# Hybrid decoder block on one core: softmax of query tiles placed between value products, two heads' operands in SBUF

## Chip, cores and metric

The kernel runs on one core of one Trainium2 chip. The metric is device time in microseconds (us), the median of several executions. One further execution was taken with the hardware profiler; the views quoted below come from it. Engines carry the profile's names: PE is TensorE (PEld its weight load), DVE VectorE, ACT ScalarE, POOL GpSimd, SP the engine that issues most DMAs.

## The reference, cut to what matters

One decoder block on 1024 tokens and 1024 channels, in fp32. After a norm and an input projection, two branches run side by side, are gated, merged and projected, and a gated ConvFFN follows. The change touches the stage in which both branches are computed.

```
# forgetting attention (FoX), 8 heads of 128
s = q_t . k_s * scale + (c_t - c_s)          # c: running sum of log forget gates; causal
o = softmax(s) @ v
# gated DeltaNet, 8 heads, in 8 chunks of 128 tokens here
S_t = exp(g_t) (I - beta_t k_t k_t^T) S_{t-1} + beta_t k_t v_t^T ;  o_t = S_t^T q_t
```

## The kernel before

The program is a row of stages: input projection with Strassen-like block products (`project`), the mixing stage (`mix`), the merge of the branches (`merge`), the output projection (`mix_out`), the ConvFFN. Products in fp32 are made of three products of high and low parts (`hi*hi`, `hi*lo`, `lo*hi`), so each operand is first split: ACT writes the high part as a cast, and POOL or DVE subtracts it to leave the low part.

In `mix` (L1276) a generator `fox` (L1246) emits the attention, one head after the other, in small steps; between its steps the loop at L1438 emits steps of two scan streams (`stream`, L1405; even heads and odd heads) and of the preparation of scan inputs (`prep`, L1287). PE follows the order in which the code is written (`manual_schedule` for PE). The other engines and the DMA queue of SP are ordered by a scheduler at build time, except where `keep_in_program_order` pins an instruction. Every engine runs its own queue in order.

A head of the attention has 8 query tiles of 128 rows, t = 0 to 7.

- `probs(h, t)` (L1174) makes one tile of probabilities. PE multiplies query and keys (three matmuls, L1187 to L1189) into a PSUM tile of `small()`; DVE adds the bias row, `cr` or, on the diagonal block, the masked `cd`, and keeps the running maximum (L1194, a pair of instructions each time); DVE negates it (L1200), ACT takes the exponential with the row sum (L1201), DVE inverts the sum and scales the tile (L1202, L1203). For t below 4 there is one score chunk, for t of 4 and more two of equal width (320, 384, 448 and 512 columns).
- `attend(h, half)` (L1206) multiplies four tiles of probabilities with the values. For each key block j, PE transposes the blocks (L1224) into a tile of `small()`, ACT and DVE split the result into `ph` and `pl` (L106, L107), and PE makes the three products with `vh`, `vl` (L1215), two key blocks later. Half 0 has 4 key blocks and tiles 0 to 3, half 1 has 8 key blocks and tiles 4 to 7.

`small()` hands out four PSUM tiles in turn, to scores, transposes, scan preparation and scan output alike. The order of a head (L1253 to L1273) is: all eight `probs`, the attend steps of half 0, then those of half 1. The four early tiles of head 0 are made in the projection (`EARLY`, L85). One set of query and key tiles (`qh`, `ql`, `kh`, `kl`), one of bias rows (`cr`, `cd`, 1024 wide) and one `vl` serve all heads. Loads of the next head's query, keys and bias are written at the first step of half 0; their split (`fox_query`, `fox_key`, L1124 to L1136) at steps 1 and 4 of half 1; the values are loaded after half 1 and split (`fox_values`, L1138) after the first chunk of tile 4.

`prep(h)` for a scan head loads eleven inputs and scales two of them on POOL (L1320: `svt` by `brk`, `skt` by `dkl`) in its first step; two further steps make the inverse's off-diagonal block (L1325 to L1333). The first `prep` is emitted at step 0 of `fox`, the scan streams begin at steps 12 and 21. In `stream` the `prep` of the next head but one is taken at steps 14, 18 and 21 of the scan.

The pool `stream2`, which holds three 512 KB tiles `wr` for weights, opens before `mix` (L449); SP loads the first three tiles of the output projection's weights into it at the start of the mixing stage.

Of the kernel before, what the change touches and what calls it, by code (L numbers as in the profile page):

```python
# [9 lines left out]
F32 = mybir.dt.float32  # L10
# [77 lines left out]
class Block:  # L88
# [322 lines left out]
    def run(self):  # L411
# [5 lines left out]
        with ExitStack() as ctx:  # L417
# [31 lines left out]
            self.st = pool(ctx, "stream2", side="right")  # L449
# [13 lines left out]
            self.mix([pool(left, f"fox{i}") for i in range(4)], pool(sc, "scan", side="right"), merge_pools)  # L463
# [11 lines left out]
            bs.close()  # L475
            banks(2, 6)
# [78 lines left out]
    def head_in(self, blk, right):  # L555
# [3 lines left out]
        with tc.tile_pool(name="hin", bufs=1) as pool, ExitStack() as px:  # L559
# [96 lines left out]
            for t in range(NT):  # L656
# [12 lines left out]
                if t == NT - 2:  # L669
# [6 lines left out]
                                   ("t2", "t3", "t1")))  # L676
# [444 lines left out]
    def fox_load_values(self, h):  # L1121
        self.fox_load(self.vl, self.vd[:, h * P:(h + 1) * P].rearrange("(t p) d -> p t d", p=P))

    def fox_query(self):  # L1124

        self.fox_parts(self.qh, self.ql)

    def fox_key(self):
        self.fox_parts(self.kh, self.kl)
# [8 lines left out]
    def fox_values(self):  # L1138
        raw = self.vl.bitcast(F32)
        self.nc.gpsimd.tensor_copy(self.vf, raw[:, 3::4, :])  # L1140
        for sl in (slice(0, 4), slice(4, 8)):

            self.tc.keep_in_program_order(self.nc.scalar.copy(self.vh[:, sl], raw[:, sl]))
            self.nc.gpsimd.tensor_tensor(self.vl[:, sl], raw[:, sl], self.vh[:, sl].bitcast(F32), ALU.subtract)

    def fox_bias(self, h):
        nc = self.nc
        nc.sync.dma_start(self.cr, self.rows_d[(H + h) * NT:(H + h + 1) * NT, :].rearrange("t c -> (t c)")
                          .partition_broadcast(P))
        nc.gpsimd.affine_select(out=self.cd.rearrange("p (n c) -> p n c", n=NT),  # L1150
                                in_=self.cr.rearrange("p (n c) -> p n c", n=NT),
                                compare_op=ALU.is_ge, fill=NEG, base=0, pattern=[[0, NT], [-1, P]],
                                channel_multiplier=1)

    def fox_first(self, pool):

        self.fox_in = pool
        self.qh, self.ql, self.kh, self.kl = (pool.tile([P, S], F32R, name=n) for n in ("qh", "ql", "kh", "kl"))
        self.cr, self.cd = (pool.tile([P, S], F32, name=n) for n in ("cr", "cd"))
        self.vl = pool.tile([P, NT, P], F32R, name="vl")  # L1160
        self.fox_load(self.ql, self.q_d[0])
        self.fox_load(self.kl, self.k_d[0])
        self.fox_bias(0)
        self.fox_load_values(0)
        yield
# [884 lines left out]
```

## Time and profile before

| | |
|---|---|
| time, median of 3 runs | 1992.53 us (1988.59 to 1996.03) |
| time of the profiled execution | 1994.26 us |
| its span | 1992.6 us |
| PE, DVE, ACT, POOL busy in the span | 96%, 75%, 54%, 48% |
| mixing stage in the span | about 812 to 1066 us |

The windows view gives, for a stretch of the span, the busy time of each engine with the count of its instructions, the clock that PE was granted as a share of full speed, the share of time in which DMA engines moved data, and GB/s. The groups view has one row per line, engine and tile: busy time, mean ns of one instruction, then the engine's idle time just before and what ended it. A timeline row is start, duration, engine, line, operation and tile. Matmuls are pipelined: the profile's duration of one is longer than the distance to the next.

### The profile page before, as it was taken

What the parts mean: (1) busy time and instruction counts of PE and PEld (TensorE: products, weight loads), DVE (VectorE), ACT (ScalarE), POOL (GpSimd) and SP (SyncE); (2) the same over time, 40 slices, a digit from 0 to 9 for tenths busy, and PEclk for the clock granted to TensorE, in tenths of its full rate; (3) what the DMA queues carried; (4) which work ended last, traced back from release to release, by engine and by line L of the source; (5) the groups of instructions that cost most, each with busy time, mean ns of one, the idle gap of its engine ahead of it and who ended that gap; (6) DMA issues with size and microseconds to landing.
All of it is one profiled execution on the core that took longest, in us unless ns stands there. A gap on an engine that the chain in (4) does not pass through costs nothing. (4 is left out here: it accounts for less than half of the span.)

```text
span 1992.6 us, 29214 instructions
## 1 busy us (share of the span) xinstructions
PE 1920.6 (96%) x9674; PEld 1605.2 (81%) x9674; DVE 1492.4 (75%) x2549; ACT 1067.5 (54%) x2383; POOL 954.3 (48%) x792
## 2 busy tenths in 40 slices
PE   8999999999999999999998999999999999999998
PEld 8988887888887777788886887877788888877886
DVE  6949887867999974487887797668877676778435
ACT  5436776763334445476765443466555555553234
POOL 2845656555555455455655043154665656530012
PEclk9999999999999999899999999999999999999999
DMA  5335556565323366766665743573433434378654
GB/s 166 96 101 164 174 189 188 185 211 206 112 106 111 112 213 257 259 222 212 230 219 203 231 137 131 188 242 124 163 126 112 148 118 136 118 250 319 211 195 160
DMA packets 191608, 350.89 MB, mean 176 GB/s; under 512 B 50784, under 2 KB 79712, under 8 KB 191456
## 3 DMA queue, kind: packets, MB, share of 16 engines
q1 hardware_dynamic: 190448, 345.35, 51.2%
q10 hardware_dynamic: 1008, 3.67, 0.5%
q8 instruction: 76, 1.25, 0.3%
q14 instruction: 76, 0.62, 0.1%
HBM read 232.76 MB, written 116.20 MB: 175 GB/s over the span
## 5 line engine op out<-in xcount | busy, mean ns | idle before, releaser
L107 POOL TENSOR_TENSOR ol<-ws,oh 128x512 fp32r<-128x512 f32 x212 | 288.3, 1362 | 218.4 <-ACT oh L106 207.6
L107 POOL TENSOR_TENSOR ol<-wr,oh 128x512 fp32r<-128x512 f32 x165 | 230.4, 1399 | 271.0 <-ACT oh L106 213.9
L106 ACT CAST oh<-ws 128x512 fp32r<-128x512 f32 x212 | 131.0, 618 | 178.3 <-PE mm L159 172.4
L106 ACT CAST oh<-wr 128x512 fp32r<-128x512 f32 x201 | 121.5, 615 | 107.7 <-PE mm L159 74.2
L205 DVE TENSOR_TENSOR ws<-wr 128x512 f32<-128x512 f32 x106 | 99.1, 935 | 103.2 <-DMA wr<-in_w_up_dram 70.5
L390 DVE SCALAR_TENSOR_TENSOR cv<-c,fw,cv 128x512 f32<-128x512 f32 (+2 forms) x176 | 127.5, 748 | 10.0 <-ACT cv L385 8.5
L390 DVE SCALAR_TENSOR_TENSOR cv<-c,cw,cv 128x511 f32<-128x511 f32 (+2 forms) x144 | 105.9, 748 | 7.4 <-ACT cv L385 5.8
L1038 DVE TENSOR_TENSOR invt<-invz 128x399 f32<-128x399 f32 (+50 forms) x114 | 94.7, 845 | 0.3
L264 ACT COPY x<-mm 128x512 f32<-128x512 f32 x158 | 91.7, 581 | 4.5 <-PE mm L159 4.5
L159 PE MATMUL mm<-b22h,oh 128*128 128x512 f32 x216 | 86.1, 399 | 7.4 <-ACT x L264 7.3
L159 PE MATMUL mm<-bt1h,oh 128*128 128x512 f32 x216 | 85.2, 395 | 5.1 <-ACT x L264 5.1
L107 DVE TENSOR_TENSOR ol<-wd,oh 128x512 fp32r<-128x512 f32 x66 | 46.3, 706 | 57.5 <-ACT oh L106 57.4
L159 PE MATMUL mm<-bt4h,oh 128*128 128x512 f32 x216 | 84.8, 393 | 4.4 <-DVE c L311 4.4
L159 PE MATMUL mm<-b11h,ol 128*128 128x512 f32 x216 | 86.2, 399 | 0.7 <-POOL ol L107 0.7
L159 PE MATMUL mm<-b11h,oh 128*128 128x512 f32 x216 | 85.8, 397 | 1.0 <-ACT oh L106 1.0
L159 PE MATMUL mm<-b11l,oh 128*128 128x512 f32 x216 | 86.4, 400 | 0.0
L159 PE MATMUL mm<-b22l,oh 128*128 128x512 f32 x216 | 86.0, 398 | 0.0
L159 PE MATMUL mm<-b21l,oh 128*128 128x512 f32 x216 | 86.0, 398 | 0.0
L159 PE MATMUL mm<-bt4l,oh 128*128 128x512 f32 x216 | 85.7, 397 | 0.0
L159 PE MATMUL mm<-bt2l,oh 128*128 128x512 f32 x216 | 85.1, 394 | 0.3 <-DVE bt2l L107 0.3
L159 PE MATMUL mm<-bt1l,oh 128*128 128x512 f32 x216 | 84.9, 393 | 0.0
L159 PE MATMUL mm<-b21h,oh 128*128 128x512 f32 x216 | 84.9, 393 | 0.0
(426 smaller groups left out, 6381.0 us busy)
## 6 DMA issues: line engine op xcount, KB each, us to landing
wr<-in_w_up_dram SPq DMA_DIRECT2D x43, 512.0 KB, 3.6
wr<-in_w_gdn_dram SPq DMA_DIRECT2D x24, 512.0 KB, 3.8
wr<-in_w_out_dram SPq DMA_DIRECT2D x24, 512.0 KB, 3.9
s<-hy SPq DMA_DIRECT2D x44, 256.0 KB, 3.0
s<-z SPq DMA_DIRECT2D x44, 256.0 KB, 3.9
wd<-in_w_down_dram SPq DMA_DIRECT2D x44, 256.0 KB, 5.7
b22h<-s SPq DMA_DIRECT2D x44, 256.0 KB, 2.9
b22l<-s SPq DMA_DIRECT2D x44, 256.0 KB, 3.3
```

Source lines behind the costliest of these rows:

```text
L106: cast = nc.scalar.copy(hi, src)
L107: (lo_eng or nc.vector).tensor_tensor(lo, src, hi.bitcast(F32), ALU.subtract)
L159: self.nc.tensor.matmul(ps, lhs[:, sl], rhs[:, k, :], start=(first and k == 0 and i == 0), stop=(k == 3 and i == 2), skip_group_check=True)
L205: v.tensor_tensor(t, x, y, op)
L264: nc.scalar.copy(t, x)
L390: nc.vector.scalar_tensor_tensor(t[:, lo:], c[:, 512 * j + lo - s:512 * (j + 1) - s], w[:, n - 1 - s:n - s], t[:, lo:], op0=ALU.mult, op1= ...
L1038: nc.vector.tensor_tensor(tv, z[:, m:n, 0:n].to_broadcast([P, r, n]), z[:, m, c0:c1].unsqueeze(2).to_broadcast([P, r, n]), ALU.mult))
```

## The change

Five things change.

1. A head is written in one list of 26 steps: half 0's value products with the late tiles' softmax (t = 4 to 7) between them, then half 1's value products, with the next head's early tiles (t = 0 to 3) ahead of them and among them. Chunks of scores are 512 columns and the rest, which for t = 4 is 512 + 256 computed columns (128 used) and one bias instruction fewer. A tile's last part (maximum, exponential, scaling) now belongs to the step of its last score chunk.
2. Two sets of query, key and value tiles stand in SBUF, for even and odd heads, the second in a pool of its own (`other`). The bias is in halves: the lower one per set, the upper one (`crh`) and the two masked ones (`cd`) single.
3. Loads and splits of the next head move to steps 1, 3 and 5 of the 26, beside the late tiles; the split of the head's own values to step 2 (step 0 for head 0).
4. In `prep` the loads are a step of their own; POOL's scaling is the next step, and pinned in program order. The streams take `prep` at scan steps 10, 15, 18 and 21; the first stream begins at step 9, the second at step 19.
5. `stream2` opens after the merge's last pool is closed, and the three block tiles of the projection stand in another order in their pool.

```diff
-            self.st = pool(ctx, "stream2", side="right")
...
             bs.close()
+            self.st = pool(ctx, "stream2", side="right")
...
-                                   ("t2", "t3", "t1")))
+                                   ("t1", "t2", "t3")))
...
+    def fox_load_head(self, h):
+        _, ql, _, kl, _ = self.sets[h % 2]
+        self.fox_load(ql, self.q_d[h])
+        self.fox_load(kl, self.k_d[h])
+        self.fox_bias(h, 0)
...
-        w = n if t < 4 else n // 2
...
-        for lo in range(0, n, w):
+        for half, lo in enumerate(range(0, n, 512)):
...
         nc.vector.tensor_scalar(p, p, mm[:, 1:2], None, op0=ALU.mult)
         pts.append(p)
+        yield
...
         for h in range(H):
-            pts = [] if h else self.pts
-            for t in range(len(pts), NT):
-                yield from self.probs(h, t, pts)
-                if h and t == 4:
-                    self.fox_values()
-            for half in range(2):
-                for i, _ in enumerate(self.attend(h, half, pts)):
...
+            late, early = late(), early()
+            order = [first, late, late] * 4 + [first, early, early, early, last, last, last, early] + [last] * 6
+            for i, part in enumerate(order):
+                if i == 1 and more:
+                    self.fox_load_head(h + 1)
+                    self.fox_load_values(h + 1)
+                elif i == 3 and more:
+                    self.fox_query(h + 1)
+                elif i == 5 and more:
+                    self.fox_key(h + 1)
+                if i == (2 if h else 0):
+                    self.fox_values(h)
+                if next(part, DONE) is not DONE:
+                    yield
+                if i == 12:
+                    finish(first)
+                    if more:
+                        self.fox_bias(h + 1, 1)
...
-                eng = nc.gpsimd
+                yield
                 for t, f in ((vb, self.brk), (kt, self.dkl)):
                     for sl in (slice(0, 4), slice(4, 8)):
-                        eng.tensor_tensor(t[:, sl], t[:, sl], bc(f)[:, sl], ALU.mult)
+
+                        tc.keep_in_program_order(
+                            nc.gpsimd.tensor_tensor(t[:, sl], t[:, sl], bc(f)[:, sl], ALU.mult))
                 yield
...
-                        if h + 2 < H and i in (14, 18, 21):
-                            if i == 14:
+                        if h + 2 < H and i in (10, 15, 18, 21):
+                            if i == 10:
```

What this does to the queues, at three places. First PE, within a head of the steady state (the third). `p_` tiles under `ident` are transposes of probabilities for the value products, `kh,qh` and its two companions are scores, `us` are the scan. Before, the last two tiles' scores and the first transposes behind them:

```order
L1187 MATMUL ms<-kh,qh 128x448
L1188 MATMUL ms<-kl,qh 128x448
L1189 MATMUL ms<-kh,ql 128x448
L1357 MATMUL us<-ss,sqd 128x128
L1358 MATMUL us<-su,saq 128x128
L1351 MATMUL us<-sr,sxt 128x128
L1325 MATMUL ms<-sx_9190,sat 64x64 x8
L1187 MATMUL ms<-kh,qh 128x512
L1188 MATMUL ms<-kl,qh 128x512
L1189 MATMUL ms<-kh,ql 128x512
```

In the changed kernel, the same head's half 0 and its first late tile:

```order
L1242 MATMUL ms<-ident,p_9036 128x128
L1242 MATMUL ms<-ident,p_9083 128x128
L1242 MATMUL ms<-ident,p_9096 128x128
L1242 MATMUL ms<-ident,p_9156 128x128
L1203 MATMUL ms<-kh,qh 128x512
L1204 MATMUL ms<-kl,qh 128x512
L1205 MATMUL ms<-kh,ql 128x512
L1392 MATMUL us<-ss,sqd 128x128
L1393 MATMUL us<-su,saq 128x128
L1381 MATMUL us<-ss,skT 128x128
L1203 MATMUL ms<-kh,qh 128x256
L1204 MATMUL ms<-kl,qh 128x256
```

Scores used to follow scores with only scan work between; now each tile's scores stand between the transposes of two key blocks.

Second POOL, at the entry of the mixing stage, from the split of head 0's values on. `ql`, `kl` are the low parts of head 1's query and keys, `svt` and `skt` the scan inputs, first those of scan head 0. Before:

```order
L1144 TENSOR_TENSOR vl<-vl,vh 128x512 x2
L1320 TENSOR_TENSOR svt<-svt,brk 128x512 x2
L1320 TENSOR_TENSOR skt<-skt,dkl 128x512 x2
L1136 TENSOR_TENSOR ql<-ql,qh 128x512 x2
L1150 AFFINE_SELECT cd<-cr 128x1024
```

In the changed kernel:

```order
L1145 TENSOR_TENSOR vl<-vl,vh 128x512 x2
L1136 TENSOR_TENSOR ql<-ql,qh 128x512 x2
L1136 TENSOR_TENSOR kl<-kl,kh 128x512
L1153 AFFINE_SELECT cd_7828<-crl 128x512
L1355 TENSOR_TENSOR svt<-svt,brk 128x512 x2
L1355 TENSOR_TENSOR skt<-skt,dkl 128x512 x2
```

The scan inputs of head 0 used to be scaled ahead of head 1's query; now they stand behind head 1's query, half its keys and its masked bias.

Third SP at the same place: the last loads of scan head 0 and what follows. Before:

```order
L1293 DMA sqd<-qdd_1551 128x1024
L1378 DMA sgz<-gzd_1592 128x1024
L126 DMA wr<-in_w_out_dram 128x1024 x3
L1119 DMA kl<-kd_1585 128x1024
L1119 DMA ql<-qd_1577 128x1024
```

In the changed kernel:

```order
L1326 DMA sqd<-qdd_1551 128x1024
L1119 DMA ql<-qd_1577 128x1024
L1119 DMA kl<-kd_1585 128x1024
L1152 DMA crl<-rows 128x512
L1119 DMA vl<-vd 128x8x128
L1413 DMA sgz<-gzd_1592 128x1024
```

Head 1's query and keys move up by four transfers; the three weight tiles `wr` left this place for the middle of the merge.

More of the change, by code (lines that the diff above doesn't have):

```diff
@@ L461, in merge_pools @@
                 self.merge_first(pool(bs, "br0"))
-            self.mix([pool(left, f"fox{i}") for i in range(4)], pool(sc, "scan", side="right"), merge_pools)
+            self.mix([pool(left, f"fox{i}") for i in range(5)], pool(sc, "scan", side="right"), merge_pools)
             sc.close()
@@ L1155, in fox_first, with bias, fox_set @@
+    def bias(self, h, half):
+        return (self.crh if half else self.sets[h % 2][4]), self.cd[half]
+    def fox_set(self, pool):
+        return ([pool.tile([P, S], F32R, name=n) for n in ("qh", "ql", "kh", "kl")]
+                + [pool.tile([P, 512], F32, name="crl")])
+    def fox_load_head(self, h):
[3 more added lines that the diff above has]
+        self.fox_bias(h, 0)
     def fox_first(self, pool):
         self.fox_in = pool
-        self.qh, self.ql, self.kh, self.kl = (pool.tile([P, S], F32R, name=n) for n in ("qh", "ql", "kh", "kl"))
@@ L1159, in fox_first @@
[L1159 to L1163, printed above, removed]
+        self.sets = [self.fox_set(pool)]
+        self.crh = pool.tile([P, 512], F32, name="crh")
+        self.cd = [pool.tile([P, 512], F32, name=f"cd{i}") for i in range(2)]
+        self.vls = [pool.tile([P, NT, P], F32R, name="vl")]
+        self.fox_load_head(0)
@@ new lines, in fox, with late, early @@
+            more, after = h + 1 < H, []
+            first, last = self.attend(h, 0, pts), self.attend(h, 1, pts)
+            def late():
+                for t in range(4, NT):
+                    yield from self.probs(h, t, pts)
+            def early():
+                for t in range(4 if more else 0):
+                    yield from self.probs(h + 1, t, after)
+            late, early = late(), early()
+            order = [first, late, late] * 4 + [first, early, early, early, last, last, last, early] + [last] * 6
@@ L1276, in mix @@
+            for part in (first, late, early, last):
+                finish(part)
+            pts = after
     def mix(self, fp, pool, before_last):
@@ L1449, in mix @@
                             take(s, 1)
[L1450 removed]
+                elif i >= 9 and i % 2:
                     take(streams[0], 1)
```

88 lines of the change are left out of this document (41 added, 47 removed).

## The prediction

> **What bounds the kernel now.** I read the page first, then stretches of the mixing stage in the windows view, then the waits of PE, then rows of the groups and the timeline.
>
> ```profile
> PE 1920.6 (96%) x9674; PEld 1605.2 (81%) x9674; DVE 1492.4 (75%) x2549; ACT 1067.5 (54%) x2383; POOL 954.3 (48%) x792
> ```
>
> PE is busy in 1920.6 of 1992.6 us, so over the whole span a change can win 72 us at most. Its instructions change order in the mixing stage alone. The next rows cut that stage into its entry and its remainder, and three heads of the remainder at the place where the softmax ends. The columns are length, then busy time of PE, PEld, DVE, ACT, POOL, then PE's clock.
>
> ```profile
> core 0: us, PE busy (x) PEld busy (x) DVE busy (x) ACT busy (x) POOL busy (x), PEclk, DMA share, GB/s
> 811.90:842.60 30.70, 26.73 (x173) 22.46 (x172) 18.83 (x53) 15.11 (x34) 15.27 (x14) 0.83 0.98 337
> 842.60:1065.60 223.00, 210.07 (x1570) 191.15 (x1568) 179.58 (x639) 156.87 (x502) 123.33 (x133) 1.00 0.60 204
> ...
> 904.40:923.50 19.10, 17.58 (x123) 15.85 (x123) 18.39 (x78) 13.83 (x46) 4.85 (x5) 1.00 0.62 207
> 923.50:937.20 13.70, 12.99 (x103) 11.69 (x102) 7.89 (x17) 9.08 (x30) 10.10 (x9) 1.00 0.94 299
> 937.30:956.50 19.20, 16.73 (x141) 15.17 (x139) 18.06 (x72) 13.90 (x47) 12.92 (x16) 1.00 0.79 278
> 956.50:971.20 14.70, 14.70 (x108) 13.74 (x109) 9.48 (x21) 8.84 (x27) 11.35 (x13) 1.00 0.29 95
> ...
> 1003.40:1023.00 19.60, 17.15 (x125) 15.29 (x124) 19.04 (x76) 13.38 (x41) 14.99 (x18) 1.00 0.60 212
> 1023.00:1036.40 13.40, 13.02 (x100) 12.03 (x99) 9.07 (x18) 9.50 (x31) 6.17 (x5) 1.00 0.38 123
> ```
>
> A head alternates. In its softmax stretch (mean of three: 19.3 us) DVE is busy 18.5 us and PE idles 2.15; in its value stretch (13.9 us) DVE is busy 8.8 us and PE idles 0.36. Over the head DVE has room (27.3 of 33.2 us), only not where PE needs it. The waits of PE in the remainder say the same: they end on what DVE does for the value products or the softmax.
>
> ```profile
> PE ya L1215 <- DVE pl L107: 4.0, 4, 2.0
> PE ms L1224 <- DVE p L1203: 2.5, 4, 0.7
> PE ms L1224 <- DVE pl L107: 1.8, 3, 1.2
> ```
>
> **The steady heads.** The new list of steps moves the four early tiles of the next head out of the softmax stretch and into the value stretch. The softmax of 60 tiles on DVE costs, from 811.9 to 1065.6 us:
>
> ```profile
> L1203 DVE TENSOR_SCALAR p<-p,mm 128x640 f32<-128x640 f32 (+7 forms) x60 | 42.4, 707 | 0.2
> L1194 DVE CUSTOM_DVE_ANT_0 p<-ms,cr 128x384 f32<-128x384 f32 (+5 forms) x53 | 27.2, 513 | 0.4 <-PE ms L1189 0.4
> L1194 DVE CUSTOM_DVE_ANT_0 p<-ms,cd,mx 128x128 f32<-128x128 f32 x53 | 17.8, 339 | 0.0
> L1194 DVE CUSTOM_DVE_ANT_0 p<-ms,cr,mx 128x192 f32<-128x192 f32 (+3 forms) x32 | 16.1, 505 | 0.2
> L1194 DVE DVE_READ_ACCUMULATOR2_ANT mx<- 128x1 f32 x145 | 11.4, 79 | 0.0
> L1202 DVE RECIPROCAL mm<-mm 128x1 f32<-128x1 f32 x60 | 9.2, 153 | 1.0 <-ACT p L1201 1.0
> L1200 DVE TENSOR_SCALAR mm<-mx 128x1 f32<-128x1 f32 x60 | 8.3, 140 | 0.1
> L1201 ACT ACTIVATE p<-p,mm 128x640 f32<-128x640 f32 (+7 forms) x60 | 47.4, 790 | 10.3 <-DVE mm L1200 10.1
> L1201 ACT ACTIVATION_READ_ACCUMULATOR p<-p,mm 128x1 f32 x60 | 11.4, 190 | 0.0
> ```
>
> The seven DVE rows sum to 132.4 us, 2.2 us a tile, 17.7 us for a head's eight. The early four hold 1280 of 4608 columns, so they cost between 28% and 50% of that, 4.9 to 8.8 us; I take 6, since the columns weigh more than the fixed parts. Their scores on PE are 3 x (256 + 256 + 384 + 512) columns. Matmuls of 512 columns start 0.23 us apart:
>
> ```profile
> 844.97 0.39 PE L1187 MATMUL ms<-kh,qh 128*128 128x512 f32 x1
> 845.20 0.39 PE L1188 MATMUL ms<-kl,qh 128*128 128x512 f32 x1
> ```
>
> That makes 4224 / 512 x 0.23 = 1.9 us. So the first stretch keeps 18.5 - 6 = 12.5 us of DVE and 17.15 - 1.9 = 15.3 us of PE; the second gets 8.8 + 6 = 14.8 us of DVE and 13.6 + 1.9 = 15.5 us of PE. On ACT the early exponentials leave the first stretch (28% to 50% of 8 x 0.98 us: about 3) and the four casts of query and keys, 2.5 us at about 0.63, enter it: 13.7 - 3 + 2.5 = 13.2 us, below PE as well. PE is then the longest engine in both, and a head could be 30.8 instead of 33.2 us: 2.4 us less, 17 us over seven heads. That is one end. The other is no gain at all, for in the second stretch DVE has 95% of PE's time, and queues in strict order do not mix perfectly. PE idles 11% of a stretch with DVE at 96% and 2.6% of one with DVE at 63%; for the new shares, about 80% and 93%, I take 4% and 6% of idle time, nearer to the low row, since idle time grows mostly as the last slack goes. 15.3 x 1.04 + 15.5 x 1.06 = 32.3, a gain of 0.9 us, and a little for the lumps at the turn of the stretches that the waits show: 1.15 us a head, **-8 us** in seven.
>
> **The score chunks.** Tile 4 computes 512 + 256 columns where it computed 320 + 320: 128 more, three times, in eight heads, 128 / 512 x 0.23 x 24 = **+1.4 us** on PE. The bias instruction that goes was one of the L1194 rows (about 0.4 us and its 0.08 us reading) and lies beside PE work in the new first stretch: nothing; without that cover it would be 0.5 us a head.
>
> **The entry.** In the entry POOL, SP and PE do this (times of start and length; SP rows with the time from issue to landing):
>
> ```profile
> 817.11 2.31 POOL L1320 TENSOR_TENSOR svt<-svt,brk 128x512 f32<-128x512 f32 x2
> 820.00 2.42 POOL L1320 TENSOR_TENSOR skt<-skt,dkl 128x512 f32<-128x512 f32 x2 [0.59 <-DMA skt<-ktd]
> 834.55 2.51 POOL L1136 TENSOR_TENSOR ql<-ql,qh 128x512 fp32r<-128x512 f32 x2 [12.13 <-ACT qh L1135]
> 837.02 1.09 POOL L1150 TENSOR_SCALAR_AFFINE_SELECT cd<-cr 128x1024 f32<-128x1024 f32 x1
> ```
> ```profile
> L1378 SPq DMA_DIRECT2D sgz<-gzd x1: 319/319/319, 816.6 to 816.6; - x1
> DMA to landing us min/median/max: 7.1/7.1/7.1
> ```
> ```profile
> 815.32 0.47 PE L1187 MATMUL ms<-kh,qh 128*128 128x512 f32 x1
> ...
> 829.34 0.63 PE L1351 MATMUL us<-svt,sxt 128*128 128x128 f32 x2
> 829.77 0.63 PE L1224 MATMUL ms<-ident,p 128*128 128x128 f32 x2
> ```
>
> POOL has scaled `svt` by 819.4, ten us before PE wants it at 829.34. In the change POOL first splits head 1's query and half its keys and masks a bias. Query `ql` takes the place of `sgz` in SP's queue, so it lands at about 816.6 + 7.1 = 823.7. Then come a cast (0.6), two splits of `ql` (2.5), one of `kl` (1.3), the mask (half of 1.09), the first half of `svt` (1.2): 829.9 at the earliest, and some 2 us later if ACT, whose cast stands behind the exponential of tile 6, is late. PE is there at about 824, and behind the scan's first matmul its queue holds tile 7's scores, which it ran at 815.3 to 816.9 before. From those to the first transposes of half 1 it is scores 1.4, bias and maximum about 1, exponential and sum 1.35 or more, inverse and scaling about 1.2: near 5, so 835 to 837, against 829.77. Meanwhile PE does 3.3 us that used to come later: scores of head 1's tiles 0 to 2 (1.2), five scan products (1.1), eight small products of the next preparation (0.9). (836 - 829.8) - 3.3 is about 3; I take **+4 us**, since tile 7's chain runs through two more queues. Ends: 0, if the operands land early enough to hide it, and +8, if ACT is 2 us late and the second scan's inputs follow late as well.
>
> The clock bears on this too:
>
> ```profile
> 811.90:821.70 9.80, 7.40 (x50) 5.91 (x48) 9.12 (x36) 5.57 (x12) 6.50 (x6) 1.00 0.89 324
> 821.70:831.90 10.20, 9.55 (x44) 8.19 (x45) 4.58 (x9) 4.13 (x10) 0.72 (x1) 0.50 1.03 387
> ```
>
> PE runs at half clock for 10.2 us, after a stretch in which it was busy 76%. I leave that as it is: the new wait falls into it. [...]
>
> **The rest.** The three `wr` tiles move from the entry, where the DMA engines are full, to the merge, whose start is as full:
>
> ```profile
> 1066.00:1090.00 24.00, 16.78 (x66) 13.19 (x67) 15.96 (x20) 10.98 (x23) 16.95 (x16) 0.89 1.02 361
> ```
>
> 1.57 MB at 361 GB/s are 4.4 us if they stand ahead of awaited loads; SP issues them behind most of the merge's first loads, and they are needed after the merge: 0, end +4. The separate scaling step in `prep` gives loads more time; POOL's waits there never held PE after the entry: 0, with -1 and +2 as ends. Loads of the next head move ahead of the scan's on SP; with two sets they wait for nothing recent: 0.
>
> Sum: -8 + 4 + 1.4 = -2.6 us, 1994.3 - 2.6 = 1991.7 for an execution like the profiled one, which lay 1.7 us above the median: **1990 us**.
>
> **The rivals.** *Even spread:* the seven heads reach 30.8 us and the entry's wait hides; -17 + 1.4 gives 1977. For it: DVE's total of 27.3 us a head and the lumps of up to 2.0 us at the turn. Against it: 95% in the second stretch. Chance 0.2.
>
> *No gain in the heads:* the four PSUM tiles, which now serve scores and transposes in turn, tie PE to DVE's and ACT's latency in every step; the entry and the columns remain, 1992.5 + 5.4 = 1998. For it: idle time read on a straight line between 2.6% and 11% gives about 33.4 us a head, no gain. Chance 0.2.
>
> *Slower, by the operands:* what happens at the entry happens in each head. Casts of the next head's query and keys, in fixed order on ACT among the late exponentials, wait for their loads, and POOL's splits hold the scan's scaling. It decides when `ql` lands after the first late exponential. At 2 us in six more heads and no gain: 1998 + 12 = 2010. For it: POOL idled 12.13 us for that cast at the entry. Against it: from head 2 on the loads are issued most of a head ahead. Chance 0.1.
>
> **How the numbers follow.** The forecast has 0.5. Its own range is 1982 to 1999 (heads -14 to -3, entry 0 to +8, the merge's loads at the upper end). A measurement of this kernel can tell about 0.5%, 10 us, from no change: below 1982.6 lie the even spread and 0.07 of the others, above 2002.5 the slower rival and 0.04. So 0.27 faster, 0.59 same, 0.14 slower. The range of 1976 to 2004 leaves out most of the slower rival and the far end of the even spread.
>
> **What would show it.** Right: heads of 31.5 to 32.5 us, DVE's share even over a head, the first `svt` product at 830 to 832 with PE idle before it. Wrong: that product before 827, or heads under 31 us (even spread), or still 33 (no gain), or ACT's casts of `qh` waiting for DMA in later heads (operands).

## The result, and the profile after

The changed kernel takes 2003.67 us (median of 7 runs, 2000.92 to 2013.2); the kernel before, beside it, 1992.75 us (7 runs, 1988.59 to 1996.57). The ratio is 1.0057, with a 95% interval of 1.004 to 1.0074: slower by some 11 us, where 2.6 us less was forecast. The profiled execution has a span of 2002.0 us, 9.4 us more than before.

The page's line of busy times shows little of it; the shares are those of before to within one point:

```profile
PE 1925.5 (96%) x9674; PEld 1609.9 (80%) x9674; DVE 1499.7 (75%) x2533; ACT 1068.4 (53%) x2383; POOL 956.3 (48%) x800
```

The windows view, cut where each head's first late tile begins (heads are counted from 0; the columns are those of the prediction), has heads 2 to 5 and the last one here:

```profile
886.21:921.03 34.82, 32.14 (x233) 29.47 (x232) 28.23 (x91) 22.64 (x76) 23.90 (x29) 0.95 0.70 208
921.03:954.03 33.00, 31.70 (x249) 28.64 (x248) 27.26 (x91) 22.27 (x72) 19.59 (x21) 1.00 0.83 285
954.03:985.25 31.22, 29.99 (x222) 27.27 (x220) 26.20 (x92) 22.42 (x75) 21.09 (x26) 1.00 0.68 215
985.25:1017.03 31.78, 31.78 (x260) 29.07 (x258) 25.23 (x89) 22.04 (x72) 20.20 (x23) 1.00 0.74 232
...
1048.97:1077.79 28.82, 24.30 (x152) 22.13 (x150) 21.10 (x57) 20.04 (x56) 12.83 (x16) 0.88 0.21 74
```

Heads 4 and 5 take 31.2 and 31.8 us, with DVE at 79% to 84%: about what was forecast. Head 2 takes 34.8, with POOL busy 23.9 us of it and a lower clock (0.95), and in the last head PE idles 4.5 us and loses clock as well (0.88). The waits of PE over the mixing stage name the places:

```profile
PE us L1386 <- POOL svt L1355: 7.0, 1, 7.0
PE ms L1242 <- DVE p L1220: 5.0, 4, 3.3
PE ms L1427 <- POOL so L1422: 2.5, 1, 2.5
```

One is at the entry (7.0 us for `svt`), one in the last head (3.3 of the 5.0 us for `p`), one in head 2 (2.5 us for `so`). The waits for `pl` that the prediction quoted of before are gone from the heads behind the entry.

To see what each place is worth, PE's rows of the timeline are added up from the projection's last product on, each matmul at its spacing in the traces (0.23 us for 512 columns, 0.175 for 384, 0.12 for 256, 0.11 for 128). Where two kernels have the same sum, PE has done equally much. The table gives how many us later than before a kernel gets there, for the changed kernel and for three experiments told below. The count is good to some 0.3 us, and the row of 210 us lies just ahead of a loss.

| PE work done | before at | changed | first | twelfth | seventeenth |
|---|---|---|---|---|---|
| 24 us, entry past | 34.8 us | +6.9 | +2.4 | +2.4 | +5.3 |
| 66 us, head 2 ahead of its loss | 82.0 | +5.7 | +1.2 | +0.1 | +4.1 |
| 72 us, behind it | 88.0 | +10.4 | +5.9 | +1.8 | +8.6 |
| 200 us, last head begins | 231.2 | +6.5 | +2.0 | -2.8 | +5.0 |
| 210 us, last head's softmax | 243.5 | +4.4 | -0.1 | -4.9 | +2.9 |
| 216 us, in its half 1 | 250.5 | +9.6 | +4.9 | -0.2 | +3.7 |
| 240 us, merge under way | 285.4 | +8.1 | +4.2 | -1.8 | +9.5 |

So in the changed kernel: entry +6.9, heads up to the last -0.4 (in which head 2's loss of +4.7 lies, so the others gain 5.1), last head -2.1 in its softmax and then +5.2, start of the merge -1.5, and +1.3 for tile 4's added columns, which this count leaves out: +9.4 us, the difference of the spans.

**The entry.** POOL's rows and ACT's:

```profile
827.59 2.67 POOL L1136 TENSOR_TENSOR ql<-ql,qh 128x512 fp32r<-128x512 f32 x2 [10.32 <-ACT qh L1135]
830.23 1.25 POOL L1136 TENSOR_TENSOR kl<-kl,kh 128x512 fp32r<-128x512 f32 x1
831.45 0.62 POOL L1153 TENSOR_SCALAR_AFFINE_SELECT cd<-crl 128x512 f32<-128x512 f32 x1
832.05 2.03 POOL L1355 TENSOR_TENSOR svt<-svt,brk 128x512 f32<-128x512 f32 x2
```
```profile
825.87 1.04 ACT L1218 ACTIVATE p<-p,mm 128x896 f32<-128x896 f32 x1 [0.65 <-DVE mm L1217]
826.82 0.19 ACT L1218 ACTIVATION_READ_ACCUMULATOR p<-p,mm 128x1 f32 x1
826.91 1.12 ACT L1135 CAST qh<-ql 128x512 fp32r<-128x512 f32 x2
```

ACT cast head 1's query at 826.91, right behind the exponential of tile 6; POOL split query and half the keys, masked the bias, and came to `svt` at 832.05. PE took it at 833.13, having idled 6.98 us. The prediction had this chain, with 829.9 as the earliest and 2 us more if ACT came late; ACT did.

**Head 2.** POOL's rows ahead of the wait, and PE's:

```profile
895.59 1.26 POOL L1136 TENSOR_TENSOR ql<-ql,qh 128x512 fp32r<-128x512 f32 x1
...
898.55 1.28 POOL L1136 TENSOR_TENSOR kl<-kl,kh 128x512 fp32r<-128x512 f32 x1
899.78 2.44 POOL L1355 TENSOR_TENSOR skt<-skt,dkl 128x512 f32<-128x512 f32 x2
902.17 1.28 POOL L1136 TENSOR_TENSOR kl<-kl,kh 128x512 fp32r<-128x512 f32 x1
903.51 0.52 POOL L1340 MEMSET sxt<- 64x512 f32 x1
904.11 2.35 POOL L1422 TENSOR_TENSOR so<-so,srs 128x512 f32<-128x512 f32 x2
```
```profile
905.52 0.78 PE L1427 MATMUL ms<-ident,so 128*128 128x128 f32 x4 [2.55 <-POOL so L1422]
```

Three jobs meet on POOL, from 898.5 on without a gap: the split of head 3's query and keys, the scaling of the next scan inputs, and at the end the scaling `so` of a finished scan head, for which PE stands still.

**The last head.** DVE's rows after, and POOL's at the same time:

```profile
1063.06 1.00 DVE L1220 TENSOR_SCALAR p<-p,mm 128x1024 f32<-128x1024 f32 x1
1063.99 1.52 DVE L107 TENSOR_TENSOR ol<-skt,oh 128x512 fp32r<-128x512 f32 x1
1065.43 0.68 DVE L107 TENSOR_TENSOR ol<-skT,oh 128x512 fp32r<-128x512 f32 x1
1066.04 0.68 DVE L107 TENSOR_TENSOR ol<-svt,oh 128x512 fp32r<-128x512 f32 x1
1066.64 1.75 DVE L107 TENSOR_TENSOR ol<-saq,oh 128x512 fp32r<-128x512 f32 x1
1068.31 0.34 DVE L1398 SCALAR_TENSOR_TENSOR ss<-ss,egl,us 128x128 f32<-128x128 f32 x1
1068.57 1.87 DVE L107 TENSOR_TENSOR pl<-ms,ph 128x512 fp32r<-128x512 f32 x3
```
```profile
1062.48 2.48 POOL L1422 TENSOR_TENSOR so<-so,srs 128x512 f32<-128x512 f32 x2
1066.25 1.59 POOL L1432 TENSOR_TENSOR yge<-yge,sgz 128x512 f32<-128x512 f32 x1 [1.28 <-ACT yge L1431]
```

The last head has no next head whose early tiles could stand between tile 7's scores and half 1, so tile 7's chain lies bare: PE idles from 1060.8 to 1064.1 and then runs at half clock (0.51) to 1069.9. Two more things end at the same place: POOL's first half of `so` (1063.7), and DVE's `pl` splits, which the build-time order has put behind four splits `ol` for the merge. Before, these stood behind the head's last split:

```profile
1062.37 0.42 DVE L107 TENSOR_TENSOR pl<-ms,ph 128x256 fp32r<-128x256 f32 x1 [0.22 <-ACT ph L106]
1064.72 0.98 DVE L107 TENSOR_TENSOR ol<-skt,oh 128x512 fp32r<-128x512 f32 x1 [1.93 <-ACT oh L106]
```

### The profile page after: what moved, and what is told of

It is laid out like the page before. It is cut to its first block, busy times and chain, and to the rows that moved or that the text cites. A ratio compares the mean times of both kernels' runs of the same rounds, so it can differ in the third digit from the quotient of the medians.

```text
span 2002.0 us, 29181 instructions
## 1 busy us (share of the span) xinstructions
PE 1925.5 (96%) x9674; PEld 1609.9 (80%) x9674; DVE 1499.7 (75%) x2533; ACT 1068.4 (53%) x2383; POOL 956.3 (48%) x800
## 5 line engine op out<-in xcount | busy, mean ns | idle before, releaser
L159 PE MATMUL mm<-bt3l,oh 128*128 128x512 f32 x216 | 84.8, 392 | 0.0
## 6 DMA issues: line engine op xcount, KB each, us to landing
s<-hy SPq DMA_DIRECT2D x44, 256.0 KB, 3.3
s<-z SPq DMA_DIRECT2D x44, 256.0 KB, 3.6
wd<-in_w_down_dram SPq DMA_DIRECT2D x44, 256.0 KB, 5.7
b22h<-s SPq DMA_DIRECT2D x44, 256.0 KB, 3.0
b22l<-s SPq DMA_DIRECT2D x44, 256.0 KB, 3.3
```

Of the source, the lines that this page charges most:

```text
L159: self.nc.tensor.matmul(ps, lhs[:, sl], rhs[:, k, :], start=(first and k == 0 and i == 0), stop=(k == 3 and i == 2), skip_group_check=True)
```

## The experiments

All are versions of the changed kernel except the sixth, which is the kernel before with one part. The time of a run scatters by some 5 us, so besides the ratio to the kernel before (five rounds each) the length of the mixing stage in the profiled execution is given, from the projection's last product to the merge's first: 255.8 us before, 265.8 changed. That length is of one execution each. Nine of the versions run the changed kernel's code at the entry and come out of it 5.3 to 7.4 us behind the kernel before, so a difference of 2 us between two stages says little unless the count of PE's work shows where it arises.

| | edit | mixing stage, us | ratio (95%) |
|---|---|---|---|
| 1 | head 1's splits later | 261.1 | 1.0042 (1.0027 to 1.0056) |
| 2 | last head's softmax ahead | 266.0 | 1.0049 (1.0031 to 1.0066) |
| 3 | `so` transposes later | 265.9 | 1.0053 (1.0033 to 1.0073) |
| 4 | softmax in one piece | 281.1 | 1.0115 (1.0096 to 1.0133) |
| 5 | part 4 undone | 265.6 | 1.0049 (1.0035 to 1.0062) |
| 6 | before, with part 4 alone | 257.6 | 1.0015 (1.0004 to 1.0026) |
| 7 | 1, and head 1's early tiles later | 261.3 | 1.0031 (1.002 to 1.0043) |
| 8 | 4, and splits back beside half 1 | 269.0 | 1.008 (1.0066 to 1.0093) |
| 9 | splits one head ahead | 264.1 | 1.0049 (1.0033 to 1.0065) |
| 10 | 9 and 1 | 261.1 | 1.001 (0.9993 to 1.0028) |
| 11 | 10 and 3 | 263.6 | 1.0037 (1.002 to 1.0055) |
| 12 | 10, splits three steps later | 256.0 | 1.0011 (0.9997 to 1.0024) |
| 13 | 2 and 3 | 263.7 | 1.004 (1.0026 to 1.0054) |
| 14 | 2, and the last `so` transposes later | 264.2 | 1.0047 (1.003 to 1.0063) |
| 15 | 12 and 14 | 257.9 | 1.0008 (0.9997 to 1.002) |
| 16 | merge's first loads later | 266.7 | 1.0058 (1.0042 to 1.0075) |
| 17 | 14 and 16 | 266.7 | 1.0072 (1.0051 to 1.0093) |
| 18 | 12 and 17 | 258.6 | 1.0011 (1.0 to 1.0022) |

**1. The entry.**

```diff
-                if i == 1 and more:
+                if i == (1 if h else 5) and more:
...
-                elif i == 3 and more:
+                elif i == (3 if h else 7) and more:
...
-                elif i == 5 and more:
+                elif i == (5 if h else 9) and more:
```

> The changed kernel, with head 1's loads and the split of its query and keys four steps later (steps 5, 7 and 9 instead of 1, 3 and 5, for head 0 alone), so that POOL scales the first scan's svt and skt ahead of that split. Theory A (the entry is lost to POOL's order: PE idled 6.98 us at 826.15 to 833.13 for svt, and the chain of tile 7 stood behind it): the first svt product starts right after the value products, at 826 to 827, and the kernel is 3 to 7 us faster than the changed one, 1997 to 2001. Theory B (svt only hides another wait of the same length: the operands of head 1 land after 824 and PE needs them next): PE idles as long a few matmuls later, and the time stays at 2002 to 2005.

The mixing stage is 4.7 us shorter and stays so to its end (its column in the table). The first `svt` product comes 13.8 us after the projection's last product instead of 21.1. By this and by the count theory A holds. The time alone would not tell: its median, 2003.13 us, lies in theory B's range, and the interval of the ratio overlaps that of the changed kernel. What is left of the entry's loss is a wait of PE for head 1's keys, in the waits of this kernel:

```profile
PE ms L1204 <- POOL kl L1136: 2.8, 1, 2.8
```

**7. The rest of the entry.** As the first, and for head 0:

```diff
+            if h == 0:
+                order = [first, late, late] * 4 + [first] + [last] * 4 + [early, last] * 4 + [last] * 2
```

> The changed kernel with head 1's loads and splits four steps later, as in the first experiment, and head 1's early tiles four value steps later in head 0 alone, so that PE has half 1's first products to do while POOL splits head 1's keys (PE idled 3.04 us for them at 830.42 in that experiment). Theory A (the entry's remaining loss is that wait): the mixing stage is 2 to 3 us ahead of the first experiment from 850 on, ratio 1.002 to 1.004. Theory B (tile 7's chain ahead of half 1 is then exposed instead, about 5 us of which 1.5 are covered): no better than the first experiment, 1.004 to 1.006.

261.3 us against 261.1: by the stage theory B. (The ratio, 1.0031, lies in theory A's range, but its interval overlaps that of the first.) With the early tiles gone from there, PE idles 2.58 us for tile 7 at 828.48 instead. The early tiles had been the cover for tile 7's chain, and the keys their price.

**4. The mix itself.** The softmax of heads 1 to 6 in one piece:

```diff
+            if 0 < h < H - 1:
+                order = [late] * 8 + [first] * 5 + [last] * 10 + [early] * 4
```

> The changed kernel, with the softmax of heads 1 to 6 in one piece again (four late tiles ahead of half 0, four early tiles of the next head behind half 1, nothing between value products); two sets, loads, splits and the scan inputs' scaling as in the changed kernel. Theory A (mixing softmax into the value products gained some 7 us in the steady heads, hidden by three losses elsewhere): 5 to 9 us slower than the changed kernel, 2009 to 2013, and its heads at about 33 us. Theory B (the mix gained nothing in the heads): 2002 to 2006.

15.3 us longer, more than theory A had. Mixing gains; but 15 us is more than the kernel before could lose by having no mix, so something else in the new set-up punishes a softmax in one piece.

**8. The splits.** As the fourth, with the splits of the next head's query and keys at steps 14 and 17 in heads 1 to 6:

```diff
-                elif i == 3 and more:
+                elif i == (14 if 0 < h < H - 1 else 3) and more:
...
-                elif i == 5 and more:
+                elif i == (17 if 0 < h < H - 1 else 5) and more:
```

> The changed kernel with the softmax of heads 1 to 6 in one piece, as in the fourth experiment, and besides with the split of the next head's query and keys back beside half 1's value products in those heads. Theory D (the softmax in one piece is 12 us slower here than in the kernel before because ACT and POOL split the next head's operands among the late exponentials): 5 to 12 us faster than the fourth experiment, ratio 1.006 to 1.009, and heads at about 33 us. Theory E (the splits are no load on the path; the scan inputs or the set-up of the chunks cost it): within 3 us of it, 1.010 to 1.013.

12.1 of the 15.3 us come back: theory D. A part of it can be read from the groups of DVE, its scaling of the probabilities, over the 48 tiles of heads 1 to 6; first the fourth, then the eighth:

```profile
L1220 DVE TENSOR_SCALAR p<-p,mm 128x128 f32<-128x128 f32 (+7 forms) x48 | 36.2, 757 | 0.1
```
```profile
L1220 DVE TENSOR_SCALAR p<-p,mm 128x128 f32<-128x128 f32 (+7 forms) x48 | 30.3, 632 | 0.2
```

757 ns a tile beside POOL's splits, 632 without them: 0.12 us on the engine that bounds a softmax in one piece, 6 us over 48 tiles. That ACT's casts make up the other 6 us is not shown.

The eighth is also the better measure of the mix. It and the twelfth below both keep the splits out of the late softmax, one with the softmax in one piece, one with it mixed in: from 24 to 200 us of PE's work the eighth loses some 1.5 us against the kernel before, and the twelfth gains 5.2.

**3. Head 2's wait.**

```diff
-                        if i in (1, 6, 8):
+                        if i in (1, 8, 10):
```

> The changed kernel, with a finished scan head's output transposes taken two scan steps later (steps 8 and 10 instead of 6 and 8), so that POOL has more time to scale them. Theory A (head 2 lost 4.7 us at 905.5, of which 2.55 us are a wait for POOL's scaling of so at the end of a full POOL queue, and the rest half clock behind it): the wait goes and nothing takes its place, 3 to 5 us faster, 1998.5 to 2000.5. Theory B (POOL stays behind through the head: svt, skt or the next wait on POOL takes over): at most 1 us, 2002.5 to 2004.

The wait for `so` is gone and the mixing stage as long as in the changed kernel (265.9): theory B. By the count some 3 of head 2's 4.7 us are won at that place and lost again within two heads (+7.1 against +6.9 at 150 us of work). In its place stand waits of the scan for ACT's copies, 0.6 us once before and now

```profile
PE us L1381 <- ACT so L1403: 3.6, 5, 1.3
```

**9, 10. Splits one head ahead.** Each set is free as soon as its head's tile 7 has its scores, so head h + 2 can be loaded and split beside half 1 of head h (`fox_load_qk` holds the two loads of `fox_load_head`):

```diff
-                if i == 1 and more:
-                    self.fox_load_head(h + 1)
+                if i == (1 if h == 0 else 1) and more:
+                    if h == 0:
+                        self.fox_load_qk(1)
+                    self.fox_bias(h + 1, 0)
...
-                elif i == 3 and more:
+                elif i == 3 and h == 0:
...
-                elif i == 5 and more:
+                elif i == 5 and h == 0:
...
+                elif i == 13 and h + 2 < H:
+                    self.fox_load_qk(h + 2)
+                elif i == 16 and h + 2 < H:
+                    self.fox_query(h + 2)
+                elif i == 19 and h + 2 < H:
+                    self.fox_key(h + 2)
```

The tenth has head 1's steps as in the first experiment: 5, 7 and 9.

> The changed kernel with query and keys of head h + 2 loaded and split beside half 1 of head h (into the set that head h has just done with) instead of those of head h + 1 among head h's late softmax; the entry as in the changed kernel. Theory D (splits among the late exponentials hold the heads back, as in the eighth experiment, here less since PE has other work): the loss of 3.3 us at head 2 goes with POOL's crowd there, the mixing stage takes 259 to 263 us instead of 265.8, ratio 1.002 to 1.0045. Theory F (with softmax mixed into the value products the splits cost nothing where they are; the crowd on POOL moves with them): 264.5 to 267 us, ratio 1.005 to 1.007.

> The ninth experiment together with the first: head 1's loads and splits four steps later, those of later heads beside half 1 of the head before last. If both effects are separate, the mixing stage is 4 to 5 us shorter than in the ninth: by theory D 254.5 to 258.5 us, ratio 0.9995 to 1.002, about the kernel before; by theory F 260 to 262, ratio 1.003 to 1.0045.

264.1 and 261.1 us: neither theory cleanly. POOL's crowd at head 2 is gone, but there is a new wait one head earlier. In the ninth it costs about 1 us; in the tenth it takes all that was won (by the count +6.2 at 72 us of work, against +5.9 in the first). ACT's and PE's rows of the tenth:

```profile
869.51 1.14 ACT L1135 CAST qh<-ql 128x512 fp32r<-128x512 f32 x2 [2.61 <-DMA ql<-qd]
870.55 0.58 ACT L106 CAST ph<-ms 128x512 fp32r<-128x512 f32 x1
```
```profile
871.96 1.11 PE L1373 MATMUL ms<-sx,sat 64*64 64x64 f32 x16 [2.82 <-issue]
```

The cast of head 3's query (the twelfth's expectation names head 2 by mistake), fixed in ACT's order, waits for its load; the value products' cast `ph` stands behind it. PE's row names no releaser, but DVE's split `pl` of that tile, held up 3.21 us by `ph`, ends at 871.85, just ahead of PE's start. This is the prediction's third rival, made by an experiment; in the changed kernel itself no cast of a later head waits for its load.

**12. The same, three steps later** (19 and 22 instead of 16 and 19):

> The tenth experiment with the splits three steps later (steps 19 and 22 of a head instead of 16 and 19). In the tenth PE lost 4.6 us at 872, where ACT's cast of head 2's query, pinned in its order, waited until 869.45 for its load (landed 869.43), and the value products' casts stood behind it. Theory G (that wait is the operands' rival of the prediction, and goes when the load has time): the mixing stage takes 256 to 258.5 us instead of 261.05, ratio 0.999 to 1.0005, as fast as the kernel before. Theory H (the splits at the end of half 1 now hold the next head's first late tile, or POOL's crowd at head 2 comes back): 260 to 263 us, ratio 1.001 to 1.004.

Theory G by the stage: it falls by 5.1 us to 255.95, as long as before (255.8). This is the only version whose stage equals the old one, and its time cannot be told from the kernel before (1.0011, 0.9997 to 1.0024; theory G had 0.999 to 1.0005).

**5, 6. Part 4 (scan inputs).** Undone in the changed kernel, and done alone in the kernel before:

```diff
-                yield
                 for t, f in ((vb, self.brk), (kt, self.dkl)):
                     for sl in (slice(0, 4), slice(4, 8)):
-                        tc.keep_in_program_order(
-                            nc.gpsimd.tensor_tensor(t[:, sl], t[:, sl], bc(f)[:, sl], ALU.mult))
+                        nc.gpsimd.tensor_tensor(t[:, sl], t[:, sl], bc(f)[:, sl], ALU.mult)
...
-                        if h + 2 < H and i in (10, 15, 18, 21):
+                        if h + 2 < H and i in (14, 18, 21):
...
```

> The changed kernel with its fourth part undone: loads and scaling of a scan head are one step again, the scaling is not pinned in program order, the streams take it at scan steps 14, 18 and 21 and begin at steps 12 and 21; softmax between value products, two sets, loads and splits stay. Theory A (part 4 costs only at the entry, by what stands ahead of svt on POOL): the first svt product moves to 826 to 830, ratio to the kernel before 1.002 to 1.005 (the changed kernel: 1.0057). Theory C (the pinned scaling and the earlier steps crowd POOL in every head, and POOL sets the pace): 8 to 12 us faster than the changed kernel, ratio 0.999 to 1.001.

> The kernel before with the fourth part of the change alone: loads of a scan head and its scaling as two steps, the scaling pinned, scan steps 10, 15, 18 and 21, streams from steps 9 and 19. Theory A (the pin hurts only where the next head's splits can move ahead of it, and these stand late in the kernel before): ratio 0.999 to 1.001. Theory C (part 4 crowds POOL in every head): 1.003 to 1.005.

Undone, the entry loses 3.6 us instead of 6.9, and the stage is no shorter (265.6), since later heads lose as much, above all to the values' split on POOL:

```profile
PE ya L1233 <- POOL vl L1145: 3.4, 2, 3.0
```

Theory A's sign did not come: the first `svt` product stands 20.8 us behind the projection (21.1 in the changed kernel), since the streams begin later in PE's order. But POOL has scaled `svt` by 820.5, and PE no longer waits for it; the ratio, 1.0049, is in theory A's range. Alone in the kernel before, part 4 costs 1.8 us of the stage, a ratio of 1.0015, between the two theories' ranges; PE waits 2.4 us for `svt` and 1.9 us for `so` there. So part 4 is not the cause by itself, and theory C falls in both. Which of its pieces does harm or good (the pin, the scan steps, the earlier start of the streams) was not separated.

**2, 13 to 18. The last head.** Second and thirteenth:

```diff
+            if not more:
+                order = [first, late, late] + [first] + [late] * 6 + [first] * 3 + [last] * 10
```

> The changed kernel, with the last head's late softmax written ahead of three of its value steps of half 0, so that these stand between tile 7's scores and half 1's transposes. Theory A (the last head has no next head to fill the gap; PE idled 3.33 us for tile 7 at 1064.12 and ran at half clock until 1070): the wait falls under 1.5 us, the half clock behind it goes, 3 to 5 us faster than the changed kernel, 1998.5 to 2000.5. Theory B (DVE is the limit in the last head, so the wait only moves ahead into its softmax): gain of at most 1 us, 2002.5 to 2004.

> The changed kernel with the edits of the second and the third experiment together: the last head's late softmax ahead of three value steps, and scan output transposes two scan steps later. In the second, tile 7 was ready 2 us earlier than in the changed kernel, but PE then waited 2.47 us for POOL's scaling of so, which ended at the same place. Theory A (two waits end together there, and each alone gains nothing): both gone, the mixing stage takes 261 to 263.5 us instead of 265.8, ratio 1.0025 to 1.0045. Theory B (DVE's pace in the last head sets it whatever PE waits for): 265 to 266.5 us, ratio 1.005 to 1.007.

Alone it gains nothing (266.0): tile 7 is ready 2 us earlier, and PE then waits for `so`. In the thirteenth that wait was to go and did not, since these last transposes are written at another place, so its 263.7 us don't answer the question. In the waits of the second:

```profile
PE ms L1429 <- POOL so L1424: 4.8, 2, 2.5
```

The fourteenth moves that place, the fifteenth does so in the twelfth:

```diff
-                for _ in range(0 if s else 3):
-                    take(prev, 1)
+                for k in range(0 if s else 5):
+                    if k not in (1, 2):
+                        take(prev, 1)
                     yield
```

> The changed kernel with the last head's late softmax ahead of three value steps, as in the second experiment, and the output transposes of the last even scan head two scan steps later, so that POOL's scaling of so, for which PE waited 2.47 us in the second and 2.46 us in the thirteenth, is done when PE gets there. Theory A (two waits end at the same place in the last head): both gone, and the half clock behind them, the mixing stage takes 261 to 263 us instead of 265.8 (266.0 in the second), ratio 1.002 to 1.0045. Theory B (DVE's pace sets the last head; splits of half 1 behind DVE's work for the merge take over): 264.5 to 266.5 us, ratio 1.0045 to 1.007.

> The twelfth experiment (mixing stage 255.95 us) with the two edits of the fourteenth. Theory A: 251 to 253 us, ratio 0.997 to 0.9995, faster than the kernel before. Theory B: 254.5 to 256.5 us, ratio 0.9995 to 1.0015, no different from the twelfth.

264.2 us, and 257.9 against the twelfth's 256.0: little or nothing. `so` is out of the way, and now PE waits for DVE, which does the merge's splits first:

```profile
PE ya L1233 <- DVE pl L107: 3.3, 2, 2.8
```

The sixteenth moves the merge's first loads, and with them these splits, behind the head's own; the seventeenth has all three edits, the eighteenth all three in the twelfth (with step 199):

```diff
-                if i == 180:
+                if i == 198:
```

> The changed kernel with the merge's first loads written at step 198 instead of 180, so that DVE's four splits of the merge's first tiles stand behind the last head's splits for its value products (as in the kernel before) and not ahead of them. Theory A (three waits end together in the last head: tile 7, POOL's so, DVE's merge splits): alone this gains at most 1.5 us, the mixing stage takes 264.5 to 266 us, and up to 3 us can be lost where the merge starts, if its loads land late. Theory B (DVE's four splits alone hold the last head: in the fourteenth experiment PE waited 3.09 us behind them): 261 to 263 us, ratio 1.0025 to 1.0045.

> The fourteenth experiment and the sixteenth together (loads at step 199): the last head's softmax ahead, so's transposes later, the merge's splits on DVE behind the head's. Theory A: none of the three waits is left, the mixing stage takes 259.5 to 262 us instead of 265.8, ratio 1.002 to 1.004. Theory B (a limit by DVE, or the merge's late loads, takes it back): 263.5 to 266 us, ratio 1.004 to 1.006.

> The twelfth experiment (head 1's loads later, later heads' splits one head ahead; mixing stage 255.95 us) with the three edits of the seventeenth. Theory A: 250 to 253 us, ratio 0.997 to 0.9995, faster than the kernel before. Theory B: 254.5 to 257 us, ratio 0.9995 to 1.0015.

By the stage none gains: 266.7 us alone, 266.7 with all three. The count of equal work tells more. Between 210 and 216 us of work the changed kernel loses 5.2 us, the second experiment 5.4, the fourteenth 3.7, the sixteenth 2.5 and the seventeenth 0.8. (The seventeenth also leaves the entry 1.6 us ahead of the changed kernel, though its edits are in the last head; why is not shown.) So the softmax ahead does nothing while the other two waits stand, the merge's splits alone are half of the loss (more than theory A allowed), and with all three edits nearly all of it goes. But then the merge's first product waits 8.0 us, for loads that now land too late, as ACT's rows of the seventeenth show:

```profile
1069.85 0.62 ACT L106 CAST oh<-skt 128x512 fp32r<-128x512 f32 x1 [2.23 <-DMA skt<-in_w_branch_dram]
...
1075.45 0.62 ACT L106 CAST oh<-saq 128x512 fp32r<-128x512 f32 x1 [1.52 <-DMA saq<-in_w_branch_dram]
```

So what is won in the head is given back at the merge (258.6 us in the eighteenth, too). Whether early loads with late splits would keep it was not tried.

**11** joins the third's edit to the tenth:

> The tenth experiment together with the third: a finished scan head's output transposes two scan steps later. If a wait for POOL's scaling of so is left in the tenth, it goes: 1 to 3 us shorter, 253 to 257 us by theory D. If none is left, or ACT's queue takes its place as in the third experiment, the tenth's time within 1 us.

263.6 us, 2.5 longer than the tenth, and neither of the two that were expected. By the count it leaves the entry 3.3 us later than the tenth, with the same code there: in the 10 us from 22.7 us into the stage on, the granted clock is 0.51, and 0.79 in the tenth. Behind the entry it gains 0.8 us, with waits for ACT's copies of 3.6 us (1.7 in the tenth). So one execution each doesn't tell what the edit is worth here. No version beats the kernel before.

## Why the prediction was wrong, point by point

*What bounds the kernel, and the heads.* Mechanism right, size off. The gain of the steady heads was put at 8 us; up to the start of the last head, without head 2's loss, they gain 5.1 in the changed kernel, and 5.2 in the twelfth experiment (+2.4 to -2.8). Another 2.1 us are won in the last head's softmax, for which the sum had nothing. But for head 2 (34.8 us), heads of 31.2 to 33.0 us stand against the forecast of 31.5 to 32.5. The lengths flatter a little: a head of the changed kernel holds 29.1 us of PE's work in the count, one of the kernel before 29.4. The rival of no gain falls with the twelfth experiment against the eighth. The even spread falls too: it needed 30.8 us in every head and an entry for nothing.

*The entry.* Mechanism right, size off: +4 was taken, +6.9 came, inside the ends of 0 and +8. What I counted as an end, ACT some 2 us late behind the exponential of tile 6, is what happened: `svt` came at 833.13 instead of 830 to 832, and half 1's transposes at 840.9 instead of 835 to 837.

*The scan inputs.* Here a step failed: "POOL's waits there never held PE after the entry: 0". That was read from the old order, in which splits stood beside half 1 and the scan's scaling had POOL to itself. The change brings both into the same stretch. It was not the scaling that held PE but what came last on POOL, `so`: 4.7 us in head 2 with the half clock behind it (1.7 in the twelfth experiment, where the splits stand elsewhere). The rival of the operands had POOL's queue in it, with a wait in each of six heads; it came in one. The waits of PE before, from 842.6 us on, had a small one of this kind already, which the prediction passed over:

```profile
PE ms L1392 <- POOL so L1387: 0.8, 1, 0.8
```

*The last head.* This step was missing. I multiplied a head's gain by seven and gave the eighth zero. But the changed order lives on the next head's early tiles as cover for tile 7, and the last head has none: +5.2 us, of which its mixed softmax had won 2.1 ahead. I also left out that a scheduler orders DVE anew there, and puts the merge's splits ahead of the head's.

*Columns and weights.* The +1.3 for tile 4's columns is worked out from the spacing of matmuls, as the prediction's +1.4 was; no run has it alone. No cost of the `wr` tiles shows in the merge, whose start comes out 1.5 us cheaper.

*The clock.* I left it as it was, and at the entry that holds: the kernel before ran at half clock (0.50) for 10.2 us there, the changed one for most of 7.2 us (0.54) and for 4.1 us (0.50): by an estimate from these clocks, about 5 us lost in both. In head 2 and the last head the kernel before had full clock (1.00 from 842.6 to 1065.6 us), so there it is a loss of its own. The rows of three waits in the changed kernel, each with the stretch behind it, and ahead of them the entry's first slow stretch (the clock is the third number from the end):

```profile
817.40:824.60 7.20, 7.12 (x44) 6.01 (x45) 5.51 (x21) 2.21 (x5) 0.00 (x0) 0.54 1.01 377
...
826.15:833.10 6.95, 0.00 (x0) 0.00 (x0) 0.85 (x2) 2.92 (x6) 5.51 (x6) 0.84 1.16 267
833.10:837.20 4.10, 4.07 (x13) 3.49 (x14) 1.32 (x4) 0.27 (x1) 4.10 (x4) 0.50 1.02 386
902.80:905.50 2.70, 0.17 (x2) 0.00 (x0) 2.67 (x13) 2.60 (x12) 2.56 (x4) 1.00 0.94 313
905.50:909.50 4.00, 3.98 (x21) 3.98 (x22) 3.46 (x8) 1.17 (x2) 3.83 (x6) 0.57 0.16 58
...
1060.80:1064.10 3.30, 0.00 (x0) 0.00 (x0) 1.89 (x8) 2.79 (x6) 3.14 (x4) 0.82 0.20 79
1064.10:1069.90 5.80, 5.78 (x28) 5.78 (x29) 5.80 (x8) 3.78 (x10) 2.46 (x2) 0.51 0.12 45
```

Behind the waits of head 2 and of the last head PE runs at about half clock (0.57 and 0.51) for 4.0 and 5.8 us, which by an estimate from these clocks costs some 2 and 3 us more: head 2's 4.7 us are 2.6 of waiting and some 2 of half clock. That the lower clock costs time shows in the spacing of matmuls: of 512 columns they start 0.43 us apart at 821.20 in the changed kernel, at a clock of 0.50, and 0.23 us apart at 812.67. PE had idled 2.55 us ahead of head 2's half clock and 3.33 us ahead of the last head's. What idle time brings it on was not shown: in the kernel before PE was busy 0.53 of the 2.50 us from 953.9 on, and the clock was 1.00 there and in the 3.6 us behind.

The prediction read the kernel before too coarsely here. It had the half clock from 821.7 on behind a stretch of 9.8 us in which PE was busy 76%; in the last 3.4 of these PE was busy a third:

```profile
818.30:821.70 3.40, 1.12 (x8) 0.54 (x6) 3.40 (x14) 1.62 (x4) 2.81 (x3) 1.00 0.98 374
```

The sum, then: predicted -8 (heads) + 4 (entry) + 1.4 (columns) = -2.6; measured -5.1 + 6.9 + 1.3, and +4.7 (head 2), -2.1 and +5.2 (last head), -1.5 (merge), which makes +9.4. The terms that I had were right to 3 us; two that I had not decided the sign. The range given with the forecast, 1982 to 1999, is also narrower than the ends listed there make when they fall together (1980 to 2003).

## What to carry to other kernels

A software pipeline that hides a step behind the next item's work is priced item by item: the steady items, the first (whose operands come while everything else does) and the last, which has no next one to hide behind. When work moves, look not only at the engine it is moved for, but at what else that work issues on the side engines, and what stands last in the queue there. Where several waits end at the same place, removing one of them may gain nothing, and a null result of a single edit doesn't clear it.

## What the runs showed of the hardware

Some of DVE's instructions took longer while POOL worked. In the last head (rows above) DVE's `ol` split of one size takes 0.68 us at 1065.43, while POOL idles (1064.96 to 1066.25), and 1.52 and 1.75 us beside POOL's scaling of `so` and `yge`; the one at 1066.04, which had begun ahead of `yge`, takes 0.68 us too. In the fourteenth experiment two `ol` beside `so` take 1.44 and 1.52 us, and the one behind it 0.68. The scaling of probabilities shows the same, 757 against 632 ns in the fourth and eighth experiments. In their traces and those of before and changed, 74 scalings took over 0.1 us longer than is usual for their size, and POOL was at work beside every one; of 106 with no work of POOL beside them none did (43 and 55 of these in the traces of before and changed). The splits `pl`, whose one input lies in PSUM, keep 687 and 686 ns in the fourth and the eighth (means of 37 splits of 512 columns each).

Why the `ol` splits and the scaling took longer beside POOL and `pl` did not, no run shows. For the prediction this means that the splits that stand beside the softmax on POOL are paid on DVE too (757 against 632 ns a tile), which its sum did not have; in the changed kernel that is little, 720 ns a tile over heads 1 to 6 against 708 before.
